# Block 2's retention gate, retention projection, attention projection and merge gates: from channels on partitions to tokens on partitions

## The chip, the cores and the metric

The kernel runs on 1 core of a Trainium2 chip. The metric is device time in microseconds (us) of one execution. TensorE (PE) multiplies, VectorE (DVE) and ScalarE (ACT) do elementwise work, GpSimd (POOL) does small elementwise work and starts some DMAs, SyncE (SP) starts the weight DMAs.

## The reference, cut to what matters

Two blocks of two layers each run on 256 tokens of width 1024. The change is in the second block's mixer, which both of its layers run:

```python
z = jnp.einsum('bsd,dc->bsc', x, w_in) + b_in
q_a, k_a, v_a, q_r, k_r, v_r, g_r, gate_a, gate_b = jnp.split(z, SPLIT_POINTS, axis=-1)
...
y_b = (jax.nn.silu(g_r) * y_r.reshape(B, S, RET_V_WIDTH)).astype(x.dtype)
merged = (jax.nn.sigmoid(gate_a) * jnp.einsum('bsc,cd->bsd', y_a, w_attn_proj)
          + jax.nn.sigmoid(gate_b) * jnp.einsum('bsc,cd->bsd', y_b, w_ret_proj))
return jnp.einsum('bsd,de->bse', merged, w_out)
```

`g_r` is 2048 wide (4 retention heads of 512), `gate_a` and `gate_b` are 1024 wide, `y_a` is 384 wide, `y_b` 2048, `merged` 1024. Everything is float32.

## The kernel before

**Numbers in two parts.** Every float32 operand of a large product is written as hi + lo: hi is the value rounded to fp32r by ACT, lo the remainder taken by DVE. A product is three matmuls (hi by hi, lo by hi, hi by lo) summed in one PSUM bank. Activations lie transposed in tiles `phl` (128 channels on the partitions, then 256 tokens of hi and 256 of lo). For weights, `Weights.load` (L84 to L113) takes 128x1024 pieces: SP loads one into one of 4 buffers `wraw`, ACT writes `whi` (L102), DVE writes `wlo` (L103); `whi` and `wlo` have 6 buffers each. A raw buffer is free once its `wlo` is written, a `whi`/`wlo` buffer once PE has read it for the last time. 512 columns of a matrix with 1024 rows are 4 such pieces, and all splits stand in the instruction queues of ACT and DVE between the other work.

**Two ways to multiply.** With channels on the partitions, 128 weight columns are PE's stationary operand and the tokens move: `mm_wide` (L317 to L329) moves hi and lo of 256 tokens side by side (512 columns) against `whi`, then 256 columns against `wlo`, 8 of each for 128 output channels; `mm_dim` (L301 to L315) does the same product in three matmuls of 256 moving columns. With tokens on the partitions, 128 tokens are the stationary operand and 512 weight columns move: `mm_tok` (L259) needs 24 matmuls for 128 tokens by 512 channels (1024 rows deep), `mm_pair` (L274) writes two banks of 512 channels.

**The retention heads.** For each of 4 heads h: `ret_qk(h)`; `ret_gated(h-1)`; `ret_v(h)`; `ret_proj(h-1)`; `ret_out(h)`; `ret_gate(h)`. After the last head comes `ret_gated(3)`. Before, `ret_gate` makes the gate channel-major: four `mm_wide` into PSUM; `both` (L333 to L340) adds the two halves and the bias, first on ACT, then on DVE; two Silu on ACT. `ret_gated` transposes the normalised head output `yr` on PE (it doesn't need the gate for that), multiplies from PSUM with the gate on DVE and splits the product into `phl`. `ret_proj` (96 `mm_dim` matmuls a head) collects `y_b @ w_ret_proj` in four PSUM banks `rp` over all heads, channel-major.

**The merge.** In four chunks of 256 channels: two gates by `mm_wide` and Sigmoid; in the first chunk also `ret_proj(3)`; the attention projection by `mm_dim`; then three DVE operations (L1339 and L1340 multiply the two projections with their gates, L1341 adds) and the split into `mT`. The product is channel-major already, so PE has nothing to do for it, and goes on with the next chunk. `mT` is the stationary side of the `w_out` product (`mm_rows`, L287).

**Order.** A scheduler orders the instructions of each engine when the kernel is built; on the chip each engine then takes them strictly in that order, and waits at the first one whose inputs or buffers are not ready.

Of the kernel before, what the change touches and what calls it, by code (L numbers as in the profile page):

```python
# [22 lines left out]
KT = D // P  # L23
# [12 lines left out]
RET_HEADS = 4  # L36
# [93 lines left out]
class Net:  # L130
# [1004 lines left out]
    def layer2(self, l, xT):  # L1135
        nc, a, wk, X = self.nc, self.a, self.wk, self.X
        w_in, b_in = a["w_in_2"][l], a["b_in_2"][l]
        QA, KA, VA, QR, KR, VR, GR, GA, GB = 0, 1152, 2304, 3456, 4480, 5504, 7552, 9600, 10624
# [3 lines left out]
        ps = self.bank()  # L1142
        nc.tensor.transpose(ps[:, :NB], btmp, self.ident[:NB, :NB])
        bT = wk.tile([P, NB], F32, name="bT", tag="bT")
        nc.vector.tensor_copy(bT, ps[:, :NB])
        bias = lambda c: bT[:, c // P:c // P + 1]
# [18 lines left out]
        og = [[None] * NT for _ in range(N_GROUPS)]  # L1165
        sms = [self.small.tile([P, 3, 6], F32, name="sms", tag="sms") for _ in range(NT)]
        nms = [self.small.tile([P, 3, 6], F32, name="nms", tag="nms") for _ in range(NT)]
        for g in range(N_GROUPS):
            br = wk.tile([P, 512], F32, name="bva", tag="bv")[:, :384]
            nc.gpsimd.dma_start(br, b_in[VA + 384 * g:VA + 384 * (g + 1)].partition_broadcast(P))  # L1170
            tab = wk.tile([P, 6, S], F32, name="tab", tag="tab")
# [3 lines left out]
            get = self.w.cols(w_in, VA + 384 * g, 384)  # L1175
            if g == 0 and self.z:
                self.behind(self.z[0], *self.made(2))
            v = []
            for t in range(NT):
                ps = self.bank(self.acc)[:, :384]  # L1180
# [13 lines left out]
        yT = self.new_parts(3)  # L1194
# [4 lines left out]
        R = [dict() for _ in range(RET_HEADS)]  # L1199
# [71 lines left out]

        def ret_gate(h):
            r = R[h]
            r["g"] = wk.tile([P, 4, S], F32, name="sgr", tag="sgr")
            get = self.w.cols(w_in, GR + 512 * h, 512)
            for j in range(4):
                ps = self.wide()
                self.mm_wide(ps, xT, range(KT), get, j * P)
                self.both(r["g"][:, j, :], ps, bias(GR + 512 * h + j * P))
            for j in (0, 2):  # L1280
                nc.scalar.activation(r["g"][:, j:j + 2, :], r["g"][:, j:j + 2, :], AF.Silu)

        def ret_gated(h):
            r = R[h]
            r["yb"] = self.new_parts(4, wk)
            hi, lo, _ = r["yb"][0]
            for t in range(NT):
                ps = self.bank()
                for j in range(4):
                    nc.tensor.transpose(ps[:, j * P:(j + 1) * P], r["y"][t][:, j * P:(j + 1) * P], self.ident)  # L1290
                z = wk.tile([P, 4, P], F32, name="yz", tag="pt")
                sl = slice(t * P, (t + 1) * P)
                nc.vector.tensor_tensor(z, ps.rearrange("p (j c) -> p j c", j=4), r["g"][:, :, sl], op=ALU.mult)
                self.split(z, hi[:, :, sl], lo[:, :, sl])

        rp = []

        def ret_proj(h):
            if h == 0:
                rp.extend(self.bank(self.acc) for _ in range(4))  # L1300
            gw = self.w.rows(a["w_ret_proj_2"][l], h * 4, 4)
            for c in range(8):
                self.mm_dim(rp[c // 2][:, (c % 2) * S:(c % 2 + 1) * S], R[h]["yb"], range(4), gw, c * P,
                            start=h == 0 and c % 2 == 0, stop=h == RET_HEADS - 1, kbase=h * 4, skip_group_check=True)

        for h in range(RET_HEADS):
            ret_qk(h)
            if h:
                ret_gated(h - 1)
            ret_v(h)  # L1310
            if h:
                ret_proj(h - 1)
            ret_out(h)
            ret_gate(h)
        ret_gated(RET_HEADS - 1)
        self.drain()


        mT = self.new_parts(KT)
        wap = a["w_attn_proj_2"][l]  # L1320
        for c2 in range(4):
            s = wk.tile([P, 2, 2, S], F32, name="gate", tag="w4")
            for n, c0 in enumerate((GA, GB)):
                get = self.w.cols(w_in, c0 + 256 * c2, 256)
                for j in range(2):
                    ps = self.wide()
                    self.mm_wide(ps, xT, range(KT), get, j * P)
                    self.both(s[:, n, j, :], ps, bias(c0 + 256 * c2 + j * P))
                nc.scalar.activation(s[:, n], s[:, n], AF.Sigmoid)
            if c2 == 0:  # L1330
                ret_proj(RET_HEADS - 1)
            gp = self.w.load(wap, 0, 3, 256 * c2, 256)
            ps = self.bank()
            for j in range(2):
                self.mm_dim(ps[:, j * S:(j + 1) * S], yT, range(3), gp, j * P)
            hi, lo, _ = mT[c2 // 2]
            k0 = 2 * (c2 % 2)
            flat = lambda n: s[:, n].rearrange("p j c -> p (j c)")
            nc.vector.tensor_tensor(flat(0), ps, flat(0), op=ALU.mult)  # L1339
            nc.vector.tensor_tensor(flat(1), rp[c2], flat(1), op=ALU.mult)  # L1340
            nc.vector.tensor_tensor(flat(0), flat(0), flat(1), op=ALU.add)  # L1341
            self.split(s[:, 0], hi[:, k0:k0 + 2, :], lo[:, k0:k0 + 2, :])

        g1, b1 = self.row(a["ln1_g_2"][l]), self.row(a["ln1_b_2"][l])
        get = self.w.rows(a["w_out_2"][l], 0, KT)
        pss = [[self.bank(self.acc) for _ in range(2)] for _ in range(NT)]
        hT = self.new_parts(KT)
        z = []
# [53 lines left out]
        for n, f0 in enumerate(starts[:-2]):  # L1402
            cur = ff(starts[n + 1])
            get = self.w.rows(wd, 4 * n, 4)
# [4 lines left out]
        k0 = starts[-2] // P  # L1409
        nk = D_FF_2 // P - k0  # L1410
        get = self.w.rows(wd, k0, nk)
# [18 lines left out]
        return nT  # L1430

    def block2(self, xT, depth=DEPTH):
        b = dict(v=4, bv=1, tab=1, qaT=1, kaT=1, og=6, w4=2, pt=2, rot=3, dec=1, sc=3, yr=2, sgr=1, bT=1, retcs=1, phl=2)
        with Tags(self.tc, "wk2", b) as self.wk:
            self.retcs = self.wk.tile([P, 2, S], F32, name="retcs", tag="retcs")
            self.nc.gpsimd.dma_start(self.retcs, self.a["retcs"])
            self.qaT = self.wk.tile([P, 6, S], F32, name="qaT", tag="qaT")
            self.nc.gpsimd.memset(self.qaT, 0.0)
            for l in range(depth):
                xT = self.layer2(l, xT)  # L1440
            self.flush()
# [64 lines left out]
```

## Time and profile before

| what | value |
|---|---|
| time, median of 2 runs | 1914.88 us (1914.68 to 1915.07) |
| the profiled execution's own time | 1913.21 us |
| its span, first to last instruction | 1911.4 us |
| PE busy | 1865.5 us (98%) |
| DVE, ACT, POOL busy | 1304.1, 1035.3, 78.7 us |
| granted TensorE clock, mean | 0.994 |
| heads and merge of the first layer | about 855 to 1113 us |
| heads and merge of the second layer | about 1430 to 1690 us |

The profile's times are those of one execution, microseconds from the start of its span. A row of instructions gives start, length, engine, source line, operation, the tile written and the tiles read, shape and count; in brackets behind it stands how long the engine was idle before, and what ended that. PE's length of one matmul (0.39 us for 512 columns) includes its way through the array: the next one starts earlier, so a rate is read from start to start.

### The profile page before, as it was taken

The page shows a single profiled execution, that of the slowest core. Times are in us where ns is not written, and L with a number is a line of the kernel's source. Part 1 is how long each engine was busy: PE and PEld are TensorE (multiplying, and loading weights), DVE is VectorE, ACT ScalarE, POOL GpSimd, SP SyncE. Part 2 cuts the span into 40 slices and gives each one's busy share as a digit, 9 for nine tenths or more (in the row PEclk, how much of TensorE's full clock was granted, in tenths as well). Part 3 has the DMA queues.
Part 4 walks back from the last instruction along what each step waited for, and adds up shares of the span by engine and source line. Part 5 has one row for each costly group of instructions (what it writes and reads, how often), then busy time and mean ns, then how long its engine had stood idle before and what let it go on. Part 6 is the DMA issues. An engine that isn't in the chain of part 4 may idle for free.

```text
span 1911.4 us, 27784 instructions
## 1 busy us (share of the span) xinstructions
PE 1865.5 (98%) x10282; PEld 1605.7 (84%) x10282; DVE 1304.1 (68%) x2458; ACT 1035.3 (54%) x1745; POOL 78.7 (4%) x127
## 2 busy tenths in 40 slices
PE   8999999999999999999999999999999999999997
PEld 6787888888778888888888978888888888988886
DVE  6877656687776566667666676667568666676565
ACT  6564455555645455665555545554566555655552
POOL 2001000000000001000001000000000000000000
PEclk9999999999999999999999999999999999999999
DMA  7534575545346646564556656663564556656562
GB/s 208 165 112 135 183 251 183 192 151 156 110 152 196 207 157 188 164 190 145 178 176 212 197 177 198 198 192 119 169 191 135 175 183 197 194 175 213 188 190 89
DMA packets 187133, 334.00 MB, mean 175 GB/s; under 512 B 11623, under 2 KB 109079, under 8 KB 186613
## 3 DMA queue, kind: packets, MB, share of 16 engines
q1 hardware_dynamic: 180160, 308.94, 51.6%
q0 software_dynamic: 6528, 23.18, 4.0%
q8 instruction: 81, 1.33, 0.3%
q14 instruction: 56, 0.45, 0.1%
q10 hardware_dynamic: 308, 0.10, 0.0%
HBM read 331.10 MB, written 4.62 MB: 176 GB/s over the span
## 4 chain that ended last, share of the span: by engine, by line
PE 85%; DVE 6%; DMA 4%; ACT 2%; issue 2%; POOL 0%; SPq 0%; DVEq 0%; ACTq 0%; POOLq 0%
PE bank L325 24%; PE bank L284 21%; PE bank L268 14%; PE bank L327 12%; DVE wlo L103 2%; PE bank L386 2%; DMA wraw<-in_w_in_dram 2%; PE bank L315 2%; PE bank L314 2%; PE bank L313 2%; PE bank L419 2%; PE bank L249 1%; PE bank L411 1%; PE bank L1259 1%; ACT whi L102 1%
## 5 line engine op out<-in xcount | busy, mean ns | idle before, releaser
L103 DVE TENSOR_TENSOR wlo<-wraw,whi 128x1024 fp32r<-128x1024 f32 (+2 forms) x628 | 711.2, 1148 | 322.7 <-ACT whi L102 231.3
L102 ACT ACTIVATE whi<-wraw 128x1024 fp32r<-128x1024 f32 (+2 forms) x628 | 608.7, 997 | 346.6 <-PE bank L284 112.7
L325 PE MATMUL bank<-phl,whi 128*128 128x512 f32 x2080 | 532.2, 395 | 0.4 <-ACT whi L102 0.4
L325 PEld LDWEIGHTS bank<-phl,whi 128*128 128x128 f32 x2080 | 374.9, 189 | 69.0 <-ACT whi L102 1.2
L284 PE MATMUL bank<-whi,phl 128*128 128x512 f32 x1280 | 358.0, 395 | 1.0 <-ACT phl L230 1.0
L268 PE MATMUL bank<-whi,phl 128*128 128x512 f32 (+4 forms) x1152 | 340.3, 377 | 4.1 <-ACT phl L230 2.0
L327 PEld LDWEIGHTS bank<-phl,wlo 128*128 128x128 f32 x2080 | 284.2, 190 | 23.2 <-DVE wlo L103 2.7
L327 PE MATMUL bank<-phl,wlo 128*128 128x256 f32 x2080 | 291.7, 283 | 0.6 <-DVE wlo L103 0.6
L284 PEld LDWEIGHTS bank<-whi,phl 128*128 128x128 f32 x1280 | 237.7, 189 | 52.7 <-ACT phl L230 2.9
L268 PEld LDWEIGHTS bank<-whi,phl 128*128 128x128 f32 x1152 | 210.5, 190 | 35.3 <-ACT phl L230 4.0
L268 PE MATMUL bank<-wlo,phl 128*128 128x512 f32 (+4 forms) x576 | 214.4, 374 | 2.4 <-DVE wlo L103 2.4
L284 PE MATMUL bank<-wlo,phl 128*128 128x512 f32 x640 | 206.3, 394 | 0.1
L284 PEld LDWEIGHTS bank<-wlo,phl 128*128 128x128 f32 x640 | 120.2, 188 | 28.7 <-DVE wlo L103 2.7
L268 PEld LDWEIGHTS bank<-wlo,phl 128*128 128x128 f32 x576 | 109.0, 189 | 17.9 <-DVE wlo L103 4.4
L225 POOL TENSOR_TENSOR ry<-ry,mhalf 128x1 f32<-128x1 f32 (+1 forms) x40 | 33.8, 846 | 1285.1 <-DVE ry L224 1277.6
L315 PE MATMUL bank<-phl,wlo 128*128 128x256 f32 x304 | 86.3, 284 | 0.0
L314 PE MATMUL bank<-phl,whi 128*128 128x256 f32 x304 | 86.1, 283 | 0.0
L313 PE MATMUL bank<-phl,whi 128*128 128x256 f32 x304 | 85.5, 281 | 0.0
L230 ACT ACTIVATE phl<-bank 128x512 fp32r<-128x512 f32 (+2 forms) x62 | 33.1, 558 | 50.2 <-PE bank L249 49.6
L313 PEld LDWEIGHTS bank<-phl,whi 128*128 128x128 f32 x304 | 57.7, 190 | 0.2
L314 PEld LDWEIGHTS bank<-phl,whi 128*128 128x128 f32 x304 | 57.3, 189 | 0.2
L315 PEld LDWEIGHTS bank<-phl,wlo 128*128 128x128 f32 x304 | 57.5, 189 | 0.0
(301 smaller groups left out, 1707.9 us busy)
## 6 DMA issues: line engine op xcount, KB each, us to landing
wraw<-in_w_in_dram SPq DMA_DIRECT2D x172, 512.0 KB, 4.6
wraw<-in_w_mlp_up_dram SPq DMA_DIRECT2D x64, 512.0 KB, 4.7
wraw<-in_w_mlp_down_dram SPq DMA_DIRECT2D x64, 512.0 KB, 4.5
wraw<-in_w_ffn_gate_dram SPq DMA_DIRECT2D x44, 512.0 KB, 4.6
wraw<-in_w_ffn_up_dram SPq DMA_DIRECT2D x44, 512.0 KB, 3.9
wraw<-in_w_ffn_down_dram SPq DMA_DIRECT2D x44, 512.0 KB, 4.5
wraw<-in_w_in_dram SPq DMA_DIRECT2D x54, 384.0 KB, 3.8
wraw<-in_w_out_dram SPq DMA_DIRECT2D x32, 512.0 KB, 4.0
```

Of the source, the lines that this page charges most:

```text
L102: first = nc.scalar.activation(hi[:, :n], src, AF.Copy)
L103: ins = nc.vector.tensor_tensor(lo[:, :n], src, hi[:, :n].bitcast(F32), op=ALU.subtract)
L225: nc.gpsimd.tensor_tensor(y, y, self.mhalf[:, :n], op=ALU.pow)
L268: self.order(nc.tensor.matmul(ps, self.part(parts, kt)[x][:, sl], get(kt + kbase)[w], start=start and n == 0, stop=stop and n == len(terms ...
L284: ins = nc.tensor.matmul(pss[j], self.part(parts, kt)[x][:, sl], get(kt + kbase)[w][:, j * 512:(j + 1) * 512], start=start and n == 0, sto ...
L313: self.order(nc.tensor.matmul(ps, wh, xh, start=first, stop=False, **kw), n == 0)
L314: nc.tensor.matmul(ps, wh, xl, start=False, stop=False, **kw)
L315: nc.tensor.matmul(ps, wl, xh, start=False, stop=last, **kw)
L325: self.order(nc.tensor.matmul(flat, get(kt)[0][:, c:c + P], both, start=n == 0, stop=False), n == 0)
L327: nc.tensor.matmul(ps[:, 0], get(kt)[1][:, c:c + P], self.part(parts, kt)[0], start=False, stop=n == len(kts) - 1)
L386: nc.tensor.matmul(o, qs(h), ks(h), start=True, stop=True)
L419: nc.tensor.matmul(po[:, h * 64:(h + 1) * 64], pts[kb][:, h, :], v(kb, h), start=kb == 0, stop=kb == t)
```

## The change

All four products are made with tokens on the partitions. `ret_gate` makes, for each half t of 128 tokens, one bank by `mm_tok`, adds a bias row that POOL has spread over the partitions by DMA (`bvg`, in the same single buffer as `bvr`), and takes Silu. `ret_gated` multiplies y and gate before transposing, and splits the transposed product out of PSUM. `ret_proj` uses `mm_pair`, 48 matmuls a head. The merge runs over two halves n of 512 channels: gate a of both token halves, (for n = 0 the last `ret_proj`), gate b of t = 0, merge of t = 0, gate b of t = 1, merge of t = 1; a merge is the attention projection by `mm_tok` (9 matmuls), the three DVE operations (now L1333, L1334, L1335), and a new transpose of the sum (4 on PE, L249) with the split behind it. Two bias rows (`row`) are loaded a layer; the buffers of `sgr` are two of 512 columns in place of one of 4 x 256.

```diff
         def ret_gate(h):
             r = R[h]
-            r["g"] = wk.tile([P, 4, S], F32, name="sgr", tag="sgr")
+            br = wk.tile([P, 512], F32, name="bvg", tag="bv")
+            nc.gpsimd.dma_start(br, b_in[GR + 512 * h:GR + 512 * (h + 1)].partition_broadcast(P))
             get = self.w.cols(w_in, GR + 512 * h, 512)
-            for j in range(4):
-                ps = self.wide()
-                self.mm_wide(ps, xT, range(KT), get, j * P)
-                self.both(r["g"][:, j, :], ps, bias(GR + 512 * h + j * P))
...
+            for t in range(NT):
+                ps = self.bank()
+                self.mm_tok(ps, xT, t, range(KT), get)
+                s = wk.tile([P, 512], F32, name="sgr", tag="sgr")
+                nc.vector.tensor_tensor(s, ps, br, op=ALU.add)
+                nc.scalar.activation(s, s, AF.Silu)
+                r["g"].append(s)
...
             for t in range(NT):
...
+                z = wk.tile([P, 512], F32, name="yz", tag="pt")
+                nc.vector.tensor_tensor(z, r["y"][t], r["g"][t], op=ALU.mult)
+                self.transpose_in(z, r["yb"], t, 4)
...
+            for t in range(NT):
+                self.mm_pair(rp[t], R[h]["yb"], t, range(4), gw, start=h == 0, stop=h == RET_HEADS - 1, kbase=h * 4)
...
+        brs = [self.row(b_in[c0:c0 + D]) for c0 in (GA, GB)]
+        for n in range(2):
...
+            def gate(e, t, get):
+                ps = self.bank()
+                self.mm_tok(ps, xT, t, range(KT), get)
+                nc.vector.tensor_tensor(ss[t][:, e], ps, brs[e][:, sl], op=ALU.add)
+                nc.scalar.activation(ss[t][:, e], ss[t][:, e], AF.Sigmoid)
+
+            def merge(t):
+                ps = self.bank()
+                self.mm_tok(ps, yT, t, range(3), gp)
+                sa, sb = ss[t][:, 0], ss[t][:, 1]
+                nc.vector.tensor_tensor(sb, rp[t][n], sb, op=ALU.mult)
+                nc.vector.tensor_tensor(sa, ps, sa, op=ALU.mult)
+                nc.vector.tensor_tensor(sa, sa, sb, op=ALU.add)
+                self.transpose_in(sa, mT, t, 4, 4 * n)
...
+            get = self.w.cols(w_in, GA + 512 * n, 512)
+            for t in range(NT):
+                gate(0, t, get)
+            if n == 0:
                 ret_proj(RET_HEADS - 1)
+            get = self.w.cols(w_in, GB + 512 * n, 512)
+            gate(1, 0, get)
+            gp = self.w.load(wap, 0, 3, 512 * n, 512)
+            merge(0)
+            gate(1, 1, get)
+            merge(1)
```

The order that the scheduler made of it differs at three places that matter. Numbers behind a name tell buffers of one name apart.

On PE in the first layer, before: the end of the last head's gate and what follows (`yr` is the head's output, `10262` the first merge gate's bank).

```order
L327 MATMUL bank_10207<-phl_6957,wlo_10147 128x256 x2
L1290 MATMUL bank_10229<-ident_79,yr_10105 128x128 x4
L1290 MATMUL bank_10238<-ident_79,yr_10123 128x128 x4
L325 MATMUL bank_10262<-phl_6956,whi_10252 128x512 x4
L325 MATMUL bank_10262<-phl_6957,whi_10258 128x512 x4
```

The same place of the changed kernel (`yz` is head output times gate, `phl_10000` its transposed halves, `bank_8951` and `bank_8952` are `rp` of t = 0, `bank_10051` is the first merge gate):

```order
L268 MATMUL bank_9972<-whi_9940,phl_6957 128x512 x2
L268 MATMUL bank_9972<-wlo_9941,phl_6957 128x512
L249 MATMUL bank_10003<-ident_79,yz_10001 128x128 x4
L284 MATMUL bank_8951<-whi_10107,phl_10000 128x512
L284 MATMUL bank_8952<-whi_10107,phl_10000 128x512
L284 MATMUL bank_8951<-whi_10107,phl_10000 128x512
L284 MATMUL bank_8952<-whi_10107,phl_10000 128x512
L284 MATMUL bank_8951<-wlo_10108,phl_10000 128x512
L249 MATMUL bank_10012<-ident_79,yz_10010 128x128 x4
L268 MATMUL bank_10051<-whi_10029,phl_6956 128x512
```

The transposes now read a product of the gate, and five matmuls of `ret_proj(3)`, which read the split of the first transposes, stand between those of t = 0 and t = 1.

On PE of the changed kernel, the end of the second merge (n = 0, t = 1) and what follows (`bank_10287` is the attention projection, `gate_10026` the merged sum, `bank_10333` the next half's first gate):

```order
L268 MATMUL bank_10287<-wlo_10231,phl_8202 128x512
L268 MATMUL bank_10287<-whi_10230,phl_8202 128x512 x2
L268 MATMUL bank_10287<-whi_10236,phl_8202 128x512 x2
L268 MATMUL bank_10287<-wlo_10237,phl_8202 128x512
L249 MATMUL bank_10300<-ident_79,gate_10026 128x128 x4
L268 MATMUL bank_10333<-whi_10311,phl_6956 128x512
```

Before, the next chunk's gate followed the attention projection directly; now the four transposes stand in between. It is the same behind the first merge and the third (n = 1, t = 0); behind the fourth, 16 matmuls of the `w_out` product stand between projection and transposes.

On DVE at that second merge, before (the second chunk of 256 channels; `bank_8973` is `rp`, `bank_10611` the attention projection):

```order
L340 TENSOR_TENSOR gate_10502<-bank_10585,gate_10502 128x256
L103 TENSOR_TENSOR wlo_10741<-wraw_10738,whi_10740 128x768
L1340 TENSOR_TENSOR gate_10502<-bank_8973,gate_10502 128x512
L1339 TENSOR_TENSOR gate_10502<-bank_10611,gate_10502 128x512
L103 TENSOR_TENSOR wlo_10772<-wraw_10769,whi_10771 128x1024
L1341 TENSOR_TENSOR gate_10502<-gate_10502 128x512
```

and of the changed kernel (`row_10023` is the bias of gate b, `bank_8953` is `rp`, `bank_10287` the attention projection):

```order
L103 TENSOR_TENSOR wlo_10324<-wraw_10321,whi_10323 128x1024
L1326 TENSOR_TENSOR gate_10026<-bank_10260,row_10023 128x512
L103 TENSOR_TENSOR wlo_10330<-wraw_10327,whi_10329 128x1024
L1333 TENSOR_TENSOR gate_10026<-bank_8953,gate_10026 128x512
L1334 TENSOR_TENSOR gate_10026<-bank_10287,gate_10026 128x512
L103 TENSOR_TENSOR wlo_10390<-wraw_10387,whi_10389 128x1024
L1335 TENSOR_TENSOR gate_10026<-gate_10026 128x512
```

In both, weight splits stand inside the chain; in the changed kernel the sum at its end is what PE's transposes read. At the first and third merge, L1326, L1333, L1334 and L1335 follow each other without a split between.

## Rows read from the trace of the kernel before

**Rows 1.** The page's head, engines and granted clock over the span.
```profile
span 1911.4 us, 27784 instructions
PE 1865.5 (98%) x10282; PEld 1605.7 (84%) x10282; DVE 1304.1 (68%) x2458; ACT 1035.3 (54%) x1745; POOL 78.7 (4%) x127
```

**Rows 2.** All of PE's waits between 886 and 1112 us (total, times, longest).
```profile
PE bank L1259 <- DVE vr L1233: 0.3, 1, 0.3
```

**Rows 3.** PE's instructions in order of time: start, length, engine, line, operation.
```profile
919.87 1.07 PE L268 MATMUL bank<-whi,phl 128*128 128x512 f32 x4
920.78 0.39 PE L268 MATMUL bank<-wlo,phl 128*128 128x512 f32 x1
...
924.41 0.28 PE L313 MATMUL bank<-phl,whi 128*128 128x256 f32 x1
...
935.92 0.63 PE L1259 MATMUL bank<-vhi,scp 128*128 128x512 f32 x2
...
1047.28 1.03 PE L1290 MATMUL bank<-ident,yr 128*128 128x128 f32 x8
1048.07 1.18 PE L325 MATMUL bank<-phl,whi 128*128 128x512 f32 x4
...
1084.05 0.28 PE L313 MATMUL bank<-phl,whi 128*128 128x256 f32 x1
...
1086.20 2.00 PE L325 MATMUL bank<-phl,whi 128*128 128x512 f32 x8
1088.05 1.12 PE L327 MATMUL bank<-phl,wlo 128*128 128x256 f32 x8
```

**Rows 4.** Groups by line and shape: count, busy us, mean ns of one, idle before.
```profile
L103 DVE TENSOR_TENSOR wlo<-wraw,whi 128x1024 fp32r<-128x1024 f32 x516 | 622.6, 1221 | 281.2 <-ACT whi L102 203.5 <-PE bank L327 71.0 <-issue 1.3
L1341 DVE TENSOR_TENSOR gate<-gate 128x512 f32<-128x512 f32 x8 | 5.5, 687 | 0.0
L340 DVE TENSOR_TENSOR sgr<-bank,sgr 128x256 f32<-128x256 f32 x32 | 13.5, 421 | 26.1 <-ACT sgr L339 26.1
L102 ACT ACTIVATE whi<-wraw 128x1024 fp32r<-128x1024 f32 x516 | 530.7, 1055 | 293.6 <-PE bank L284 103.0 <-PE bank L314 66.2 <-DMA wraw<-in_w_in_dram 38.0
L1329 ACT ACTIVATE gate<-gate 128x512 f32<-128x512 f32 x16 | 10.1, 634 | 11.7 <-DVE gate L340 11.6
```

**Rows 5.** From one engine to the next, in order of time: PE to ACT, DVE to ACT.
```profile
1038.90 2.00 PE L325 MATMUL bank<-phl,whi 128*128 128x512 f32 x8
...
1039.10 0.47 ACT L339 ACTIVATE sgr<-bank,bT 128x256 f32<-128x256 f32 x1 [2.10 <-PE bank L327]
...
1085.38 0.42 DVE L340 TENSOR_TENSOR gate<-bank,gate 128x256 f32<-128x256 f32 x1
...
1085.83 0.64 ACT L1329 ACTIVATE gate<-gate 128x512 f32<-128x512 f32 x1 [0.53 <-DVE gate L340]
```

**Rows 6.** DVE at the first merge of the first layer, in order of time.
```profile
1086.58 0.69 DVE L1340 TENSOR_TENSOR gate<-bank,gate 128x512 f32<-128x512 f32 x1
1087.18 0.68 DVE L1339 TENSOR_TENSOR gate<-bank,gate 128x512 f32<-128x512 f32 x1
1087.77 1.22 DVE L103 TENSOR_TENSOR wlo<-wraw,whi 128x1024 fp32r<-128x1024 f32 x1
...
1088.90 0.69 DVE L1341 TENSOR_TENSOR gate<-gate 128x512 f32<-128x512 f32 x1
```

**Rows 7.** DMA issues: kind, queue, count, size, median us to landing.
```profile
wraw<-in_w_in_dram SPq DMA_DIRECT2D x172, 512.0 KB, 4.6
...
bvr<-in_b_in_dram POOLq DMA_DIRECT2D x8, 256.0 KB, 5.4
...
row<-in_ln_b_dram POOLq DMA_DIRECT2D x4, 512.0 KB, 6.1
```

**Rows 8.** Stretches: length, busy us (count) by engine, granted clock, DMA share, GB/s.
```profile
152.00:159.80 7.80, 5.27 (x42) 4.48 (x40) 3.71 (x12) 4.58 (x16) 1.43 (x2) 1.00 0.00 0
159.80:166.70 6.90, 5.27 (x19) 4.61 (x20) 3.97 (x6) 1.79 (x3) 2.41 (x4) 0.51 0.19 45
...
1327.00:1334.00 7.00, 4.79 (x28) 3.98 (x28) 6.59 (x12) 1.76 (x3) 0.92 (x1) 1.00 0.40 114
```

**Rows 9.** The two long idle times of PE within those stretches, by what ended them.
```profile
161.43 1.08 PE L249 MATMUL bank<-ident,mix 128*128 128x128 f32 x4 [3.13 <-DVE mix L574]
...
1331.73 0.52 PE L249 MATMUL bank<-ident,x 128*128 128x128 f32 x3 [2.15 <-DVE x L1097]
```

More of the change, by code (lines that the diff above doesn't have):

```diff
@@ L1273, in ret_gate @@
             r = R[h]
-            r["g"] = wk.tile([P, 4, S], F32, name="sgr", tag="sgr")
+            br = wk.tile([P, 512], F32, name="bvg", tag="bv")
+            nc.gpsimd.dma_start(br, b_in[GR + 512 * h:GR + 512 * (h + 1)].partition_broadcast(P))
             get = self.w.cols(w_in, GR + 512 * h, 512)
-            for j in range(4):
-                ps = self.wide()
-                self.mm_wide(ps, xT, range(KT), get, j * P)
-                self.both(r["g"][:, j, :], ps, bias(GR + 512 * h + j * P))
-            for j in (0, 2):
-                nc.scalar.activation(r["g"][:, j:j + 2, :], r["g"][:, j:j + 2, :], AF.Silu)
+            r["g"] = []
+            for t in range(NT):
[5 more added lines that the diff above has]
+                r["g"].append(s)
         def ret_gated(h):
@@ L1285, in ret_gated @@
             r["yb"] = self.new_parts(4, wk)
-            hi, lo, _ = r["yb"][0]
             for t in range(NT):
[L1288 to L1294, printed above, removed]
+                z = wk.tile([P, 512], F32, name="yz", tag="pt")
+                nc.vector.tensor_tensor(z, r["y"][t], r["g"][t], op=ALU.mult)
+                self.transpose_in(z, r["yb"], t, 4)
         rp = []
@@ L1299, in ret_proj @@
             if h == 0:
-                rp.extend(self.bank(self.acc) for _ in range(4))
+                rp.extend([self.bank(self.acc) for _ in range(2)] for _ in range(NT))
             gw = self.w.rows(a["w_ret_proj_2"][l], h * 4, 4)
-            for c in range(8):
-                self.mm_dim(rp[c // 2][:, (c % 2) * S:(c % 2 + 1) * S], R[h]["yb"], range(4), gw, c * P,
-                            start=h == 0 and c % 2 == 0, stop=h == RET_HEADS - 1, kbase=h * 4, skip_group_check=True)
+            for t in range(NT):
+                self.mm_pair(rp[t], R[h]["yb"], t, range(4), gw, start=h == 0, stop=h == RET_HEADS - 1, kbase=h * 4)
         for h in range(RET_HEADS):
@@ L1320, in layer2 @@
         wap = a["w_attn_proj_2"][l]
[L1321 to L1330, printed above, removed]
-                ret_proj(RET_HEADS - 1)
[L1332 to L1342, printed above, removed]
@@ new lines, in layer2 @@
+        brs = [self.row(b_in[c0:c0 + D]) for c0 in (GA, GB)]
+        for n in range(2):
+            sl = slice(512 * n, 512 * n + 512)
+            ss = [wk.tile([P, 2, 512], F32, name="gate", tag="w4") for _ in range(NT)]
+            def gate(e, t, get):
[15 more added lines that the diff above has]
+            if n == 0:
+                ret_proj(RET_HEADS - 1)
+            get = self.w.cols(w_in, GB + 512 * n, 512)
[4 more added lines that the diff above has]
+            merge(1)
@@ L1432, in block2 @@
     def block2(self, xT, depth=DEPTH):
-        b = dict(v=4, bv=1, tab=1, qaT=1, kaT=1, og=6, w4=2, pt=2, rot=3, dec=1, sc=3, yr=2, sgr=1, bT=1, retcs=1, phl=2)
+        b = dict(v=4, bv=1, tab=1, qaT=1, kaT=1, og=6, w4=2, pt=2, rot=3, dec=1, sc=3, yr=2, sgr=2, bT=1, retcs=1, phl=2)
         with Tags(self.tc, "wk2", b) as self.wk:
```

## The prediction

> **What bounds the kernel now.** I read the page's head first, then PE's waits in the stretch that the change touches, then single rows for rates and hand-overs. The page says that PE is busy 98% of the span [rows 1]; only its rate can be gained from, and any wait that is put on it is lost. The view of waits sharpens this for the retention heads and the merge: between 886 and 1112 us PE waited once, for 0.3 us [rows 2], and the second layer's stretch, 1464.5 to 1690, answers with the same row. So nothing is there to be won by making ACT or DVE lighter, which the change also does: their work was hidden altogether. Two questions are left: how many nanoseconds PE saves by other shapes, and whether a wait now stands where there was none.
>
> **PE's own work.** In the steady state a 512-column matmul starts every 0.2275 us (four in 0.91, from 919.87 to 920.78), the 256-column ones of `mm_dim` every 0.120 us (96 of a `ret_proj` in 11.51, from 924.41 to 935.92), and an `mm_wide` costs 1.85 for its eight wide ones (1086.20 to 1088.05) and 8 x 0.12 = 0.96 for its narrow ones, 2.81 [rows 3]. Then:
> - gates: 512 channels were 4 x 2.81 = 11.2 us and become 48 x 0.2275 = 10.9; 0.3 less, 8 times a layer (4 heads, 4 halves of merge gates): 2.3 us a layer.
> - `ret_proj`: 11.51 becomes 48 x 0.2275 = 10.92; 0.6 less, 4 heads: 2.4 us a layer.
> - attention projection: 18 narrow matmuls took 2.15 (1084.05 to 1086.20 [rows 3]), four of these a layer are 8.6; 36 x 0.2275 = 8.2; 0.4 less.
> - the merge's new transposes: eight took 0.79 (1047.28 to 1048.07 [rows 3]), four then 0.4, and I add 0.1 for changing to them and back: 4 x 0.5 = 2.0 us more a layer. The transposes of `ret_gated` are as many as before.
>
> PE saves 2.3 + 2.4 + 0.4 - 2.0 = 3.1 us a layer, 6.2 in both; without the transposes 10.2. On the narrow matmuls the row shows 2 x 0.120 against 0.2275, so 12 ns for each of the 1424 / 2 pairs that become one, some 8 of these 10 us. [...]
>
> **Waits that the change adds.** Before, PE went from one chunk's projection straight to the next chunk's gate, since the merged sum came out channel-major. Now its transposes stand directly behind the projection in PE's order, three times a layer, and PE takes its instructions in order. Durations: a split by ACT 1.05, by DVE 1.22; a 128x512 operation of DVE 0.69; Sigmoid or Silu 0.63 [rows 4], and I take the same for a copy out of PSUM. Hand-overs: a PSUM result is usable 0.2 us after the next matmul could start (PE goes on at 1038.90, ACT starts at 1039.10), DVE to ACT takes 0.03 (1085.38 + 0.42 to 1085.83) [rows 5]; I use 0.05 throughout. Clocks below start when PE is through with the last matmul of a gate.
> - *First merge.* DVE adds the bias 0.2 to 0.9, Sigmoid to 1.55, `rp` times gate to 2.3, projection times gate to 3.0, sum to 3.7; transposes at 3.75. PE's nine projection matmuls end at 9 x 0.2275 = 2.05. Wait: 1.7 us.
> - *Second merge.* In the order of DVE three splits of weights stand inside this chain, and ACT's order has two. PE gives free the buffers of gate b's four weight pieces one by one during this gate, every 1.36 us (6 matmuls). The third is free at -1.4: ACT to -0.3, DVE to 0.9, so the bias add runs 0.9 to 1.6. The fourth is free at 0: ACT to 1.05 (Sigmoid behind it, 1.65 to 2.3), DVE 1.6 to 2.8. Then the two products to 4.2, one more split to 5.4 (its piece was freed by the projection's sixth matmul, ACT has it ready at 3.4), the sum to 6.1, transposes at 6.15. Wait: 4.1 us. That a split stands between product and sum is nothing new: before, it stood there too (1087.77, and the sum only at 1088.90 [rows 6]), but PE didn't wait for that sum.
> - *Third merge:* as the first, 1.7 us.
> - *Fourth merge:* as the second, but 16 matmuls of the next product (3.65 us) fill the gap until 5.7. Wait: 0.45 us.
> - *Last head's `ret_gated`.* Before, its transposes read `yr` alone. Now: at 0 PE transposes t = 0 (its product was ready), until 0.4; DVE is in a split until 0.9 and does the bias add of t = 1 to 1.6; ACT is in a split until 1.1, copies hi to 1.7, Silu to 2.35; DVE does another split to 2.8, the lo part of t = 0 to 3.5, the product of t = 1 to 4.2. PE does two projection matmuls at 1.75, three more from 3.55 to 4.25 behind the lo part, the last transposes until 4.75. Its work in that time is 0.4 + 5 x 0.2275 + 0.5 = 2.0. Wait: 2.7 us. For heads 0 to 2 the transposes come after the next head's `ret_qk`, 4 x 2.81 = 11.2 us of PE work, and cost nothing.
>
> Sum: 1.7 + 4.1 + 1.7 + 0.45 + 2.7 = 10.65 us a layer, 21.3 in both.
>
> **What I cost at nothing, and its cover.** ACT loses four 0.47 operations a head and DVE exchanges four of 0.42 for two of 0.69 [rows 4, 5]; PE didn't wait for them. The bias rows: `bvg` is issued when `ret_v`'s last add has freed the one buffer, lands 5.4 us later [rows 7], and the first add that reads it has at least `ret_out`'s 9 and the gate's 24 matmuls before it, 33 x 0.2275 = 7.5 us; without that cover the add would wait at most those 5.4 us, in the first head alone, as the others have a projection more in between. The next `bvr` now waits for the gate's last add and still has `ret_qk` and half of `ret_v`, 11.2 + 5.5 us. On POOL's queue the normalisation's small operations stand behind `bvg`, which waits for an add that precedes them anyway. The layer norm's rows now wait for the merge's bias rows; they land 6.1 us after the last gate's add [rows 7], and the first use is behind 60 matmuls of `w_out`, 13.7 us. Weight pieces: as many bytes as before, freed earlier within a gate (piece by piece, not all in the last pass).
>
> **Sum.** 21.3 - 6.2 = +15.1 us. The profiled execution took 1913.21 (span 1911.4 and 1.8 around it): 1928.3. It lies 1.67 below the median of the runs, so for the median I predict 1930 us, 0.8% slower, which is within the 2% (38 us) that a measurement of this kernel can tell from no change.
>
> **The bounds.** No row shows PE waiting at these places, as the places are new. From below a wait is 0 if the chain is done in time; the orders exclude that for the first three merges, where the transposes follow the projection directly. With every split out of the chain each of the first three costs 1.7 and the last head about 1.4 (bias add from 0.2, Silu, product at 2.3, and the lo part behind it at 3.0 leave PE through at about 3.4, less 2.0 of work), 6.5 a layer. From above, one split more in each of the five chains adds 5 x 1.22 = 6.1 a layer. My value takes the splits that the order shows.
>
> **Rivals.**
> - *The waits are covered* (the chain is shorter than I think, or PE's queue hides it): then only PE's rates count, 1914.88 - 6.2 = 1909. For it: before, all such chains were hidden [rows 2]. Against: they were hidden because nothing on PE read their end. 7%.
> - *The chains without splits*, because the splits run ahead of the adds: 2 x 6.5 - 6.2 = +6.8, 1922. For it: ACT and DVE have slack. Against: the buffer is freed by the very gate whose add waits. 18%.
> [...]
> - *Weights come late* (the slower side). A raw buffer goes round in 4.6 + 1.05 + 1.22 = 6.9 us [rows 4, 7], four of them serve a piece every 1.7 us, and PE uses a piece in 2.7 us in the merges (ten pieces in four gates of 5.46 and two projections of 2.05, with transposes 27 us). If the in-order waits on DVE hold the splits back so that each of the five places costs one whole round, 10 x 6.9 - 6.2 = +63, 1978. It decides once DVE falls more than a gate (5.5 us) behind. Against: DVE is busy 68% [rows 1]. 5%.
>
> **Chances and range.** My sum 63%, then 7, 18, 7 and 5%. Own range of the sum: 1924 to 1938. The range 1916 to 1946 takes in the chains without splits and the clock, and leaves out the first and the last rival. Faster by over 2% needs 38 us where PE's whole saving is 10; 0.01 is left for what I don't see. Slower by over 2%, above 1953: 0.05. Within: 0.94.
>
> **What would show it.** In the changed kernel's waits of PE, L249 on the tile `gate` waits for L1335, three times a layer with about 1.7, 4.1 and 1.7 us and a fourth time below 1 us; matmuls of L284 or transposes of `yz` wait about 2.7 us for L231 and L1291 once a layer. DVE's rows at the second merge show a split between L1334 and L1335. A `ret_proj` takes 10.9 us. I am wrong if these waits are missing, if PE waits for `wlo` or `whi` over 5 us in all, or if the page shows the clock at 5 near the merges.

## The result, and the profile after

The changed kernel took 1973.4 us (median of 2 runs, 1972.74 to 1974.06) against 1914.88: the ratio is 1.0302, with a 95% interval of 1.0285 to 1.0319. That is 58.5 us slower; 15 were forecast. The prediction was wrong, and the changed time lies outside its range.

The head of the page after, to be read against [rows 1]:

```profile
span 1971.0 us, 26369 instructions
...
PE 1881.4 (95%) x9602; PEld 1584.5 (80%) x9602; DVE 1306.5 (66%) x2426; ACT 1015.4 (52%) x1681; POOL 80.1 (4%) x139
```

PE has 680 instructions fewer and its share of the span fell from 98 to 95%, so there is idle time. Its "busy" sum went up all the same, from 1865.5 to 1881.4 us, so the same kind of work took longer, and the clock is to be looked at too. The waits of PE over the whole span (columns: engine and line that waited, whom it waited for, us in total, times, longest):

```profile
PE bank L249 <- DVE yz L1291: 26.4, 6, 4.4
PE bank L249 <- DVE gate L1335: 13.0, 6, 3.5
PE bank L249 <- DVE mix L574: 6.3, 2, 3.1
...
PE bank L284 <- ACT phl L230: 3.0, 6, 1.0
...
PE bank L284 <- DVE phl L231: 2.1, 2, 1.0
```

The row on `mix` is old: it leads the same view of the kernel before, with the same figures. New are the merge's transposes that wait for the sum (L1335, 13.0 us: 3.5 at each second merge, 1.5 at the first and the third), the last head's wait for its own split (L284, 1.0 + 1.0 in each layer), and, largest of all, 26.4 us for the gated product `yz` of L1291: six times 4.4, once for each of the heads 0 to 2 in both layers. Where [rows 2] had 0.3 us between 886 and 1112, there are now 22.1 us between 886 and 1160.

Here is the first of the six, in DVE's timeline (start, duration, engine, line, operation, tiles; in brackets idle time and its end), with PE's two rows behind it:

```profile
909.58 1.23 DVE L103 TENSOR_TENSOR wlo<-wraw,whi 128x1024 fp32r<-128x1024 f32 x1 [0.40 <-ACT whi L102]
910.72 0.42 DVE L340 TENSOR_TENSOR roz<-bank,roz 128x256 f32<-128x256 f32 x1
911.05 1.22 DVE L103 TENSOR_TENSOR wlo<-wraw,whi 128x1024 fp32r<-128x1024 f32 x1
912.19 0.42 DVE L1218 TENSOR_TENSOR rou<-roz,retcs 128x256 f32<-128x256 f32 x1
912.52 0.42 DVE L1220 TENSOR_TENSOR rou<-roz,retcs 128x256 f32<-128x256 f32 x1
912.86 0.42 DVE L1221 TENSOR_TENSOR rot<-rot,rou 128x256 f32<-128x256 f32 x1
913.19 0.42 DVE L1222 TENSOR_TENSOR rot<-rot,rou 128x256 f32<-128x256 f32 x1
913.53 1.28 DVE L1291 TENSOR_TENSOR yz<-yr,sgr 128x512 f32<-128x512 f32 x2
```

```profile
909.08 0.88 PE L327 MATMUL bank<-phl,wlo 128*128 128x256 f32 x6
914.36 1.52 PE L249 MATMUL bank<-ident,yz 128*128 128x128 f32 x6 [4.40 <-DVE yz L1291]
```

PE is through with the next head's `ret_qk` at 909.96. DVE then still has two splits of weights, the first of them under way, and the end of that head's rope ahead of the product (the rope is the rotation of the head's queries and keys; its last steps are L340 to L1222), though the product's inputs belong to the head before. PE's next work, the value projection, stands behind the transposes.

With these waits the clock falls. Stretches of after (us, then busy time of each engine with its instructions, then PEclk, the granted clock, DMA share, GB/s):

```profile
905.00:912.96 7.96, 4.96 (x30) 4.21 (x28) 7.52 (x16) 2.84 (x4) 0.00 (x0) 1.00 0.66 206
912.96:919.79 6.83, 5.43 (x17) 4.69 (x18) 3.23 (x6) 1.19 (x2) 0.00 (x0) 0.50 0.40 126
919.79:926.00 6.21, 6.21 (x31) 5.22 (x31) 2.31 (x6) 1.22 (x3) 0.54 (x1) 1.00 0.00 1
...
1110.94:1114.35 3.41, 3.41 (x10) 2.68 (x9) 1.30 (x2) 0.60 (x1) 0.00 (x0) 0.50 0.81 239
...
sum 37.53, PE 33.78 PEld 28.50 DVE 18.26 ACT 9.55 POOL 0.00; mean PE 3.75 PEld 3.17 DVE 2.03 ACT 1.06 POOL 0.00
```

The clock went to half at 912.96, while PE was idle, and came back at 919.79; PE did 17 matmuls in the second stretch, at a granted clock of 0.50, and 31 in the shorter third one, at 1.00. A matmul of 512 columns started every 0.43 us in the second (two in 0.86, from 916.52 to 917.38) and every 0.23 us in the third (two in 0.45, from 925.07 to 925.52). The sum is over nine such stretches of 3.41 or 6.83 us that the kernel before doesn't have: one in or right behind each of the six waits for `yz`, one behind each second merge (1110.94 is the first layer's), and one at 1360.11. Half of the 33.78 us that PE was busy in them, 17 us, is an estimate of what the clock cost, from these rates and the 0.50. The mean granted clock gives the same size: 0.985 of 1971.0 us against 0.994 of 1911.4, so (0.015 x 1971.0) - (0.006 x 1911.4) = 18 us.

### The profile page after: what moved, and what is told of

Its sections match the earlier page's. It is cut to its first block, busy times and chain, and to the rows that moved or that the text cites. A ratio compares the mean times of both kernels' runs of the same rounds, so it can differ in the third digit from the quotient of the medians.

```text
span 1971.0 us, 26369 instructions
## 1 busy us (share of the span) xinstructions
PE 1881.4 (95%) x9602; PEld 1584.5 (80%) x9602; DVE 1306.5 (66%) x2426; ACT 1015.4 (52%) x1681; POOL 80.1 (4%) x139
## 4 chain that ended last, share of the span: by engine, by line
PE 84%; DVE 8%; ACT 3%; DMA 3%; issue 2%; POOL 0%; DVEq 0%; SPq 0%; ACTq 0%; POOLq 0%
PE bank L284 25%; PE bank L268 23%; PE bank L325 17%; PE bank L327 9%; DVE wlo L103 3%; PE bank L386 2%; PE bank L249 2%; PE bank L419 2%; DMA wraw<-in_w_in_dram 2%; ACT whi L102 1%; PE bank L411 1%; PE bank L1259 1%; ACT pr L398 1%; PE bank L1244 1%; DMA lq<-in_lambda_k_dram 0%
## 5 line engine op out<-in xcount | busy, mean ns | idle before, releaser
L103 DVE TENSOR_TENSOR wlo<-wraw,whi 128x1024 fp32r<-128x1024 f32 (+3 forms) x628 | 711.1, 1148 | 306.1 <-ACT whi L102 233.6
L102 ACT ACTIVATE whi<-wraw 128x1024 fp32r<-128x1024 f32 (+3 forms) x628 | 613.5, 998 | 332.1 <-PE bank L284 158.7
L268 PE MATMUL bank<-whi,phl 128*128 128x512 f32 (+4 forms) x1712 | 522.9, 387 | 4.2 <-ACT whi L102 2.1
L284 PE MATMUL bank<-whi,phl 128*128 128x512 f32 x1536 | 428.2, 395 | 5.1 <-ACT phl L230 3.0
L325 PE MATMUL bank<-phl,whi 128*128 128x512 f32 x1568 | 403.4, 396 | 0.2 <-ACT whi L102 0.2
L268 PEld LDWEIGHTS bank<-whi,phl 128*128 128x128 f32 x1712 | 322.6, 193 | 59.5 <-ACT phl L230 4.0
L284 PEld LDWEIGHTS bank<-whi,phl 128*128 128x128 f32 x1536 | 285.6, 189 | 68.8 <-ACT phl L230 5.4
L268 PE MATMUL bank<-wlo,phl 128*128 128x512 f32 (+4 forms) x856 | 327.9, 384 | 1.8 <-DVE wlo L103 1.7
L325 PEld LDWEIGHTS bank<-phl,whi 128*128 128x128 f32 x1568 | 282.8, 189 | 52.0 <-ACT whi L102 0.9
L284 PE MATMUL bank<-wlo,phl 128*128 128x512 f32 x768 | 246.8, 394 | 0.0
L327 PEld LDWEIGHTS bank<-phl,wlo 128*128 128x128 f32 x1568 | 214.3, 190 | 18.2 <-DVE wlo L103 2.7
L327 PE MATMUL bank<-phl,wlo 128*128 128x256 f32 x1568 | 220.3, 283 | 0.6 <-DVE wlo L103 0.6
L268 PEld LDWEIGHTS bank<-wlo,phl 128*128 128x128 f32 x856 | 164.8, 193 | 28.9 <-DVE wlo L103 4.0
L284 PEld LDWEIGHTS bank<-wlo,phl 128*128 128x128 f32 x768 | 144.1, 188 | 33.6 <-DVE wlo L103 2.5
L340 DVE TENSOR_TENSOR fs<-bank,fs 128x256 f32<-128x256 f32 x72 | 30.3, 421 | 27.8 <-ACT fs L337 27.8
L340 DVE TENSOR_TENSOR rlu<-bank,rlu 128x256 f32<-128x256 f32 x56 | 23.5, 421 | 35.8 <-ACT rlu L337 35.8
```

The source lines that it names most:

```text
L102: first = nc.scalar.activation(hi[:, :n], src, AF.Copy)
L103: ins = nc.vector.tensor_tensor(lo[:, :n], src, hi[:, :n].bitcast(F32), op=ALU.subtract)
L268: self.order(nc.tensor.matmul(ps, self.part(parts, kt)[x][:, sl], get(kt + kbase)[w], start=start and n == 0, stop=stop and n == len(terms ...
L284: ins = nc.tensor.matmul(pss[j], self.part(parts, kt)[x][:, sl], get(kt + kbase)[w][:, j * 512:(j + 1) * 512], start=start and n == 0, sto ...
L325: self.order(nc.tensor.matmul(flat, get(kt)[0][:, c:c + P], both, start=n == 0, stop=False), n == 0)
L327: nc.tensor.matmul(ps[:, 0], get(kt)[1][:, c:c + P], self.part(parts, kt)[0], start=False, stop=n == len(kts) - 1)
```

## The experiments

The theory after reading the trace: (1) `yz` takes its two buffers from the tag `pt`, which the rope of the next head (`roz`, `rou`) takes too, ahead of it in the program, so the product cannot be written until that rope is done; the transposes now stand between it and `ret_v`. (2) The merges' waits are the chain that the prediction described. (3) The clock is a price on top of both, paid for idle time. The rivals are a position or a form of work that costs by itself.

**The product in a tile of its own.** L1290 and L1291 become

```diff
-                z = wk.tile([P, 512], F32, name="yz", tag="pt")
-                nc.vector.tensor_tensor(z, r["y"][t], r["g"][t], op=ALU.mult)
+                z = r["y"][t]
+                nc.vector.tensor_tensor(z, z, r["g"][t], op=ALU.mult)
```

> The changed kernel, but the gated product is written in place into the head's own output tile instead of into a tile of the pair of buffers that the next head's rope uses; same arithmetic. Theory A (the product stands behind the next head's whole rope on VectorE, because its two buffers are those of the rope's tiles): VectorE makes the product early, the six waits of 4.4 us before the transposes of heads 0 to 2 go (26.4 us), with them most of the half-clock stretches behind them (some 12 us): 1935 us (1930 to 1941). Theory B (the position of the transposes in the program makes them late, whatever tile the product is written to): no change, 1973 us. Theory C (only the waits go, the clock is down for another reason): 1947 us.

Measured: 1934.8 us, ratio to the kernel before 1.0109 (1.0091 to 1.0127). The row for `yz` is gone from PE's waits, those for the merges stay as they were:

```profile
PE bank L249 <- DVE gate L1335: 13.0, 6, 3.5
PE bank L249 <- DVE mix L574: 6.3, 2, 3.1
```

In DVE's timeline of this kernel the product now comes right behind its gate, ahead of the rope:

```profile
897.74 0.69 DVE L1282 TENSOR_TENSOR sgr<-bank,bvg 128x512 f32<-128x512 f32 x1 [0.58 <-PE bank L268]
898.35 1.22 DVE L103 TENSOR_TENSOR wlo<-wraw,whi 128x1024 fp32r<-128x1024 f32 x1
899.48 0.69 DVE L1291 TENSOR_TENSOR yr<-yr,sgr 128x512 f32<-128x512 f32 x1
...
901.22 0.42 DVE L340 TENSOR_TENSOR roz<-bank,roz 128x256 f32<-128x256 f32 x1
```

Nothing but the tile changed, the statement stands where it stood, and the second product, the one shown (`yr` L1291), ran some 14 us earlier (899.48 against 913.53 and later). Theory A held and B fell. The gain, 37 us by the two ratios (38.6 by the medians), is larger than the 26.4 us of waits, so C fell too: the clock was part of it. The six half-clock stretches at these waits hold 23.6 us of busy PE; half of that, 11.8 us, and the 26.4 us make 38.2.

**The transposes at another place.** The tile stays in `pt`; a head's transposes are put behind the next head's value projection.

```diff
-            if h:
-                ret_gated(h - 1)
             ret_v(h)
             if h:
+                ret_gated(h - 1)
                 ret_proj(h - 1)
```

> The changed kernel with the transposes of a head's gated product put behind the next head's value projection instead of ahead of it; the buffers are those of the changed kernel, so VectorE still makes the product behind the rope. Theory A (the product is late on VectorE, and TensorE has nothing else in its order meanwhile): the value projection's matmuls, 11 us, hide the product, the six waits of 4.4 us go: 1935 us (1929 to 1944), though the product still stands behind the rope in VectorE's row. Rival (the half clock and the waits come from the length of the rope itself, so that the value projection's own results then wait): above 1950 us.

Measured: 1940.3 us, ratio 1.0136 (1.0117 to 1.0155). DVE makes the product as late as ever, behind the rope, but PE reaches it later still, and no wait for `yz` is left:

```profile
916.80 0.42 DVE L1222 TENSOR_TENSOR rot<-rot,rou 128x256 f32<-128x256 f32 x1
917.13 1.29 DVE L1291 TENSOR_TENSOR yz<-yr,sgr 128x512 f32<-128x512 f32 x2
```

```profile
925.64 1.04 PE L249 MATMUL bank<-ident,yz 128*128 128x128 f32 x8
```

The 5.5 us over the kernel with the own tile are clock for the most part: the two profiled executions lie 9.2 us apart, and their mean clocks, 0.989 of 1940.4 us against 0.993 of 1931.2, make 7.8 us of it. How much of that belongs to the change was not shown. In the first layer's heads, a head takes 48.8 us here, 48.45 with the own tile and 49.06 in the kernel before (from one head's transposes to the next head's; the clock of the kernel before was 1.00 from 855 to 1050). So the late product costs next to nothing by itself, 0.4 us a head at most; it costs where PE's next instruction reads it. The two repairs agree: in the kernel before, the product was written to `pt` as well, but PE's transposes read `yr`, and what waited for the product was `ret_proj`, behind `ret_v`.

**The gate as before, the rest as changed.** `ret_gate` and `ret_gated` are those of the kernel before; the diff of the change has them.

> The changed kernel with the retention gate and the gated product as before the change (feature-major gate, transpose first and multiply behind it), the projections and merge gates as changed. Theory A: the waits of heads 0 to 2 (27.4 us), the last head's (4.7 us in two layers) and the clock behind them (some 12 us) go, the merges' 14 us stay; the gates' matmuls of 1.8 us a layer more come back: 1933 us (1927 to 1940). Rival (the added time is spread over the new matmul forms and not in the gate's chain): above 1955 us.

Measured: 1932.1 us, ratio 1.0093 (1.0073 to 1.0114). PE's waits for `gate` are there with 13.1 us, none for `yz`. **The gate alone changed, the rest as before** is the other half of this:

> The kernel before the change with only the retention gate and the gated product changed (the same product buffers as in the changed kernel), projections and merge as before. Theory A: the six waits of 4.4 us (27.4 us), the clock behind them (some 12 us), the last head's wait (2.4 us a layer) come, less 3.6 us of gate matmuls: 1955 us (1948 to 1962). Rival (the waits come of the retention projection's new form or of the merge): under 1930 us.

Measured: 1961.7 us, ratio 1.0253 (1.0238 to 1.0269); the upper end of what theory A gave, and the rival fell. Its row says why it is at the upper end:

```profile
PE bank L249 <- DVE yz L1291: 33.5, 8, 4.4
```

It is eight waits, not six: with the merge of before behind it, the last head's transposes waited for their product too, 33.5 - 26.4 = 7.1 us in two layers. In the changed kernel that place cost 2 x 2.0. Behind the first layer's wait the clock fell as well (0.50 for 3.41 us from 1071.23), which it did not do there in the changed kernel (1.00 from 1040 to 1075). The two halves, 0.93% and 2.53%, add up to 0.44% (8.4 us) more than the 3.02% of the whole change; the waits are 3.1 us of it, and a fall of 3.41 us in each layer would be 3.4 (half of it, twice, an estimate).

**The merge's transposes later.** A merged tile goes on a list, and its transposes are issued behind the matmuls of the next gate or product:

```diff
-                self.transpose_in(sa, mT, t, 4, 4 * n)
+                pend.append((sa, t, n))
...
             for t in range(NT):
                 gate(0, t, get)
+                turn()
...
             gate(1, 1, get)
+            turn()
             merge(1)
+        turn()
```

> The changed kernel, with the transposes of each merged tile put behind the matmuls of the next gate or product, so that they no longer stand right behind the sum. Theory A (the three waits of a layer at the merges, 1.67 + 3.66 + 1.67 us, are the time between the attention product and the sum on VectorE): the waits go, 14.0 us in two layers, and the half-clock stretch behind the second one with them (some 3.4 us): 1956 us (1952 to 1961); the waits of heads 0 to 2 stay as they are, 4.4 us each. Rival (the merges wait for the gates' sigmoids or for weights, and what is deferred waits elsewhere): over 1965 us.

Measured: 1956.0 us, ratio 1.0219 (1.0203 to 1.0235), as theory A had it. Between 886 and 1150 PE waits 13.2 us for `yz`, as in the changed kernel, and no longer for `gate`. The gain (17.4 us by the medians, 15.9 by the ratios) is larger than the 13.0 us of waits, as it would be if the half-clock stretches behind the second merges went too (3.4 us, half of 3.41 in each layer, an estimate).

**Work in place of the idle time.** In the changed kernel, `ret_gated` of heads 0 to 2 begins with 20 matmuls whose result nothing reads:

```diff
+            if h < RET_HEADS - 1:
+                ps = self.bank()
+                for i in range(20):
+                    kt = i % KT
+                    nc.tensor.matmul(ps, self.part(xT, kt)[0][:, :P], xT[kt // 4][2][:, kt % 4].rearrange("p a s -> p (a s)"),
+                                     start=i == 0, stop=i == 19)
```

> The changed kernel with 20 matmuls of 512 columns that nothing reads (4.55 us at 0.2275 us each) in TensorE's order between the next head's rope projections and the transposes that wait, for heads 0 to 2; VectorE's chain is untouched. Theory A (the waits are VectorE's chain, and the idle time itself brings the clock to half behind it): the matmuls fill the six waits of 4.4 us and cost about nothing, the clock stays full behind them, and some 12 us of slow matmuls go: 1962 us (1958 to 1967). Rival (the clock falls for another reason, such as the new gate's order of work): 1973 us or a little more. Rival 2 (the waits are TensorE's own, not VectorE's): the matmuls come on top, 27 us: over 1990 us.

Measured: 1964.2 us, ratio 1.0263 (1.0249 to 1.0277), 9.2 us under the changed kernel (7.5 by the ratios) although PE has 120 matmuls more. The first fill and the transposes behind it, and the granted clock of two stretches:

```profile
910.83 4.72 PE L1293 MATMUL bank<-phl 128*128 128x512 f32 x20
915.39 1.23 PE L249 MATMUL bank<-ident,yz 128*128 128x128 f32 x8
```

```profile
910.00:920.00 10.00, 10.00 (x53) 8.25 (x52) 6.74 (x12) 2.78 (x5) 0.00 (x0) 1.00 0.44 141
965.00:975.00 10.00, 10.00 (x49) 8.08 (x48) 5.33 (x11) 1.20 (x2) 0.00 (x0) 1.00 0.35 105
```

The same two stretches of the changed kernel:

```profile
910.00:920.00 10.00, 5.64 (x18) 4.86 (x19) 6.19 (x11) 1.75 (x4) 0.00 (x0) 0.66 0.41 120
965.00:975.00 10.00, 5.60 (x22) 4.73 (x21) 6.62 (x11) 2.32 (x4) 0.00 (x0) 0.66 0.43 135
```

The fill took the place of the wait and the clock stayed at 1.00, where it was 0.66 with the gap. At the first layer's second merge, where nothing was filled in, it still fell (0.50 for 6.83 us from 1104.90). Both rivals fell.

**Both repairs, and then the last head too.** First the own tile and the later transposes together:

> The changed kernel with both repairs at once: product in place in the head's output tile, and each merged tile's transposes behind the next matmuls. Theory A (the two causes stand apart and their prices add): 1934.8 less 17.4 us, 1917 us (1913 to 1922); what is left over the kernel before is the last head's wait of 2.4 us a layer. Rival (the repairs share their gain, because a wait moves on to the next place): over 1925 us.

Measured: 1917.6 us, ratio 1.0020 (1.0011 to 1.0029). The prices add. What is left in the stretch of the change are the last head's two waits:

```profile
PE bank L284 <- DVE phl L231: 1.0, 1, 1.0
PE bank L284 <- ACT phl L230: 1.0, 1, 1.0
PE bank L1259 <- DVE vr L1233: 0.4, 1, 0.4
```

In the last kernel the product is made in place behind its `Silu` in `ret_gate`, and the last head's transposes stand behind the first merge gate's matmuls:

```diff
                 nc.scalar.activation(s, s, AF.Silu)
+                nc.vector.tensor_tensor(s, r["y"][t], s, op=ALU.mult)
...
-        ret_gated(RET_HEADS - 1)
         self.drain()
...
                 gate(0, t, get)
                 turn()
+                if n == t == 0:
+                    ret_gated(RET_HEADS - 1)
```

> As the one with both repairs, and besides the last head's transposes stand behind the first merge gate's matmuls (the product is written in place into the gate's tile, behind its Silu). Theory A (all added waits are covered, the smaller TensorE work of some 3.6 us is left): 1917 less 4.7 us, 1912 us (1907 to 1916), faster than the kernel before by 0 to 0.3%. Rival (the new forms cost more than their matmuls save): 1917 us or more.

Measured: 1911.8 us, ratio 0.9988 (0.9980 to 0.9997), the fastest of all: 2.2 us under the 1914.0 that the kernel before took beside it. Between 886 and 1112 PE waits as little as in [rows 2], and its busy time, with 9602 instructions as in the changed kernel, is now below that of [rows 1]:

```profile
PE bank L1259 <- DVE vr L1233: 0.3, 1, 0.3
```

```profile
PE 1863.1 (98%) x9602; PEld 1573.9 (82%) x9602; DVE 1305.8 (68%) x2426; ACT 1013.5 (53%) x1681; POOL 80.2 (4%) x139
```

So the added time is accounted for by runs. By the ratios, each against the kernel before on its own chip, of the 3.02% (58 us) the product's tile is 1.93% (37 us), the merge's transposes 0.89% (17 us), the last head 0.32% (6 us), and 0.12% (2.3 us) come back in the last kernel.

The profiles allow the same account without what the clock does elsewhere: the time from PE's transposes in the first head, ahead of its gate (L249 on `og`), to the first ones behind `w_out` (L249 on `x`). In the first layer of the kernel before, and of the last kernel:

```profile
885.60 0.82 PE L249 MATMUL bank<-ident,og 128*128 128x128 f32 x6
1134.67 0.60 PE L249 MATMUL bank<-ident,x 128*128 128x128 f32 x4
```

```profile
885.21 0.82 PE L249 MATMUL bank<-ident,og 128*128 128x128 f32 x6
1132.41 0.60 PE L249 MATMUL bank<-ident,x 128*128 128x128 f32 x4
```

| kernel | first layer, us | second layer, us | both, us |
|---|---|---|---|
| before | 249.07 | 249.06 | 498.1 |
| changed | 278.65 | 277.34 | 556.0 |
| own tile | 258.25 | 260.17 | 518.4 |
| own tile, later merge transposes | 251.34 | 251.39 | 502.7 |
| last kernel | 247.20 | 247.19 | 494.4 |

That is 57.9 us for the change: 37.6 for the tile, 15.7 for the merges, 8.3 for the last head, and 3.7 back. The last kernel's runs show less than these 3.7 us, 2.3; what took the rest was not shown.

## Why the prediction was wrong

**The step that failed** is the last sentence on the last head's `ret_gated`: that for heads 0 to 2 the transposes "come after the next head's `ret_qk`, 4 x 2.81 = 11.2 us of PE work, and cost nothing". It compared PE's 11.2 us with the product's inputs and never asked where the product stands in DVE's row. That row has it behind the rope, whose last steps need the last matmuls of just that `ret_qk`: the work that was to cover the product was what it waited for. With the transposes behind the value projection another 11 us of PE's work do cover it; with an own tile it needs no cover. This step cost 37 of the 58 us, 26.4 of them waits and the rest the clock behind them.

**The clock** stands among the chances with 7%, and it came true besides. Behind the second merges it fell (3.41 us at 0.50 in both layers, so 1.7 us each, an estimate), behind the last head not; the six new waits, which the prediction did not have, brought most of the rest. Full matmuls ahead of the wait did not keep the clock up: at the first layer's second merge PE had started one of 512 columns every 0.23 us (1104.54 to 1105.67), and the clock was 0.50 from 1110.94. What the range's upper end, 1946, allows for the clock was the author's estimate, and no run shows it; by the trace of the changed kernel it was these 1.7 us a layer at the merges.

**The merges** were right in mechanism and nearly in size: 1.7, 4.1, 1.7 and 0.45 us were forecast, the waits read 1.5, 3.5, 1.5 and none. DVE's rows at the second merge are the forecast order, two products, a split, the sum, and PE's transposes at its end; the first row is the first merge's:

```profile
1098.79 0.66 PE L249 MATMUL bank<-ident,gate 128*128 128x128 f32 x4 [1.51 <-DVE gate L1335]
...
1107.39 0.68 DVE L1333 TENSOR_TENSOR gate<-bank,gate 128x512 f32<-128x512 f32 x1
1107.99 0.68 DVE L1334 TENSOR_TENSOR gate<-bank,gate 128x512 f32<-128x512 f32 x1
1108.59 1.22 DVE L103 TENSOR_TENSOR wlo<-wraw,whi 128x1024 fp32r<-128x1024 f32 x1
...
1109.72 0.69 DVE L1335 TENSOR_TENSOR gate<-gate 128x512 f32<-128x512 f32 x1
...
1110.46 0.71 PE L249 MATMUL bank<-ident,gate 128*128 128x128 f32 x4 [3.50 <-DVE gate L1335]
```

Later transposes gave back 17 us by the ratios (15.7 in the table) where the terms for the merges were 2 x 7.95 = 15.9: the waits a little smaller, the clock on top. **The last head** was right in mechanism: PE waited for the split of its first transposes, on ACT and then on DVE, as forecast. The 2.7 us a layer read 2.0. Moving it gave 5.7 in two layers by the medians and 8.3 in the table, 5.4 forecast; the nearness is in part luck, as the kernel it was moved in had a fall of the clock behind that place in the first layer (0.50 for 3.41 us from 1048.06), which the forecast left out.

**PE's saving** was mis-sized: 6.2 us forecast, 3.7 measured in the table where all added waits are gone (by the runs 2.3, 0.6 to 3.8 by the interval). Two of its terms can be read: a gate's 48 matmuls took the forecast 10.93 us, but a `ret_proj` took 11.16, not 10.92,

```profile
943.30:954.23 10.93, 10.93 (x50) 9.01 (x48) 5.81 (x13) 5.38 (x6) 1.11 (x2) 1.00 0.51 162
985.19:996.35 11.16, 11.16 (x50) 9.05 (x48) 6.29 (x7) 5.10 (x6) 0.54 (x1) 1.00 0.72 220
```

so the forecast was 0.24 a head too good, 1.9 over the eight; and four `mm_wide` of the kernel before, 512 channels of merge gates from 1086.20, took 11.18, so that 512 channels of a gate save 0.25 instead of the 0.29 that the forecast took, 0.6 less over the sixteen. That leaves 6.2 - 1.9 - 0.6 = 3.7. (The forecast's own figures, 4 x 2.81 and 48 x 0.2275, differ by 0.32, so its 2.3 a layer for the gates should have been 2.6.) The wide matmul of the projection starts every 0.2325 us; one rate had been taken for both forms. It changes its bank at every step, but that alone is not the reason: in the kernel before, the `w_out` product does the same, and there 32 such matmuls took 7.26 us, 0.227 each:

```profile
1114.71 1.98 PE L284 MATMUL bank<-whi,phl 128*128 128x512 f32 x8
...
1121.97 0.62 PE L284 MATMUL bank<-whi,phl 128*128 128x512 f32 x2
```

What makes the projection slower stayed open.

**Weights coming late** did not happen: no row of PE's waits after names `wlo` or `whi` in the changed stretch. The bias rows are not among them either.

## What to carry to other kernels

When an operation becomes the one that the bound engine reads next, look up where it stands in its own engine's row and what it must wait for there, its output buffer first; counting how much work lies ahead of it on the bound engine is not enough, as that work may be its own input. A tile that is taken from a shared tag after someone else's tiles, where the tag has no buffer left, can start no earlier than they end; writing in place into an input took 37 us off here. A wait of some 4 us on a TensorE that is otherwise busy should be priced with the half clock behind it (here 26.4 us of waits became 37). And a rate that was read from one form of matmul is only an estimate for another (0.2275 us against 0.2325 here).

## What the runs showed of the hardware

- In the changed kernel the clock fell to half with each of the six waits of 4.4 us and both of 3.5 us, though PE had worked without a pause ahead of them (4.96 of the 4.96 us from 905.00 to 909.96). Twice it fell during the wait, and the stretch lasted 6.83 us; the other six times it fell 0.3 to 0.5 us after the wait's end, for 3.41 us. In the kernel with the fill the stretch at the first layer's second merge lasted 6.83 us (0.50 from 1104.90 to 1111.73), where it was 3.41 in the changed one; what sets the length stayed open.
- Shorter waits are not regular: behind 2.1 us of idle PE (L249 for L1097, before 1360.11) the clock fell in the changed kernel (0.50 for 3.41 us); behind 2.2 us at the same place it did not in the kernel before [rows 8, 9] (matmuls of 384 columns stand ahead of both). Behind the last head's two waits of 1.0 us it fell in the kernel with both repairs, in the first layer, and not in the changed one (1.00 from 1040 to 1075):

```profile
1048.06:1051.47 3.41, 3.41 (x12) 2.73 (x11) 0.69 (x1) 1.88 (x2) 0.00 (x0) 0.50 0.58 219
```

Such a fall costs 1.7 us (half of 3.41, an estimate). They also come in a part of the program that the change leaves alone, near 160 and 530 us, for 6.8 to 6.9 us each: at 159.8 and 528.4 in the kernel before, at 158.6 and 527.2 in the changed one.
